# A hybrid decoder trunk on one core: fixed instruction order in the recurrence, later bank copies, branch tiles split in place, ordered loads in the last branch

## The chip, the cores and the metric

The kernel runs on one core of a Trainium2 chip. The time is device microseconds of one execution; the median of three runs of the kernel before is 1837.7 us (1836.87 to 1839.22). A core has five engines that run at the same time: TensorE (PE: matmuls, with PEld for its weight loads), VectorE (DVE), ScalarE (ACT), GpSimd (POOL) and SyncE (SP, which here issues most of the DMA loads). Each engine works through its own instructions in the order in which they were put; waits between engines go by semaphores.

## What is computed

One layer for 1024 tokens of width 1024, in fp32:

```python
h = rms_norm(x)
P = h @ w_in                       # all branches' inputs and the branch gates
y_a = rwkv7(P[...])                # 8 heads x 64, a recurrence over time
y_b = stick_breaking_attention(P[...])   # 8 heads x 64, causal
y_m = cross_attention(P[...], mem)       # 4 heads x 128, 256 memory tokens
merged = sum_b sigmoid(G_b) * (y_b @ w_branch[b])
x = x + merged @ w_out
x = x + conv_ffn(rms_norm(x))      # up, causal convolution of width 3, SwiGLU, down
```

## The kernel before, in words

**Precision.** Each fp32 operand of a large matmul is split into a high half (an fp32r copy, on ACT) and a low half (the rest, on DVE or POOL), and a product is three matmuls: high with high, high with low, low with high (`mm3`). For weights, `load_w` (L75) loads a 128x1024 tile by SP into one of two "wr" buffers, and `split_raw` (L80) makes the halves: ACT copies (L81), POOL subtracts (L82).

**Two streams.** A main stream (preparation of the recurrence, stick-breaking attention, memory attention, the recurrence `stage2`, then `group_norm`) is woven with a filler stream, the "pump": projections, gates, and the products of branches 1 and 2. Both are Python generators. `weave` (L1771) takes one step of the main stream, then so many of the filler (2.08 in `stage2`, 1.0 in `group_norm`). A filler step is one of the eight (or four) depth steps of a product: six matmuls of 512 columns. So the matmuls of both streams alternate in the traced program.

**What sets the order on an engine.** A planner orders each engine's instructions when the kernel is built, by its own estimates of when each is ready and by a priority that follows the trace. `pinned` (L108) puts an edge from an instruction to the one traced just before it on the same engine. An unpinned instruction in between can be moved forward, and then the pinned one behind it is no longer held behind the pinned ones before it. All matmuls go through `pinned`. Of the others, some do (the recurrence's copies and state updates L530, L538, L548, L550, the norm's squares L580), some do not (gate copies L755 and products L756, branch products L1162, weight splits L81 and L82, all loads).

**The recurrence** (`stage2`, L475) has 16 chunks of 64 tokens, each in three main steps: matmuls for A and a DVE copy per head pair (`v1`, L530); matmuls for W and ACT copies (L538); matmuls for Y and the new state, DVE updates of the state (L548), and eight ACT copies into y (L550). Each chunk takes the four PSUM banks of tag "g"; a chunk's first matmuls need the banks that the chunk before it held until its y copies were done. After chunks 3, 7, 11, 13 and 15 `norm_part` (L567) takes means (L573, L574), squares (L580, sixteen or eight) and normalizations (L589) of the finished part between the steps.

**Filler items.** `proj_item` runs eight depth steps into two of the four "mm" banks, and `fin` copies the banks out in the same step as the last six matmuls. For a gate (`gate_item`, L749) `fin` is two ACT copies (L755) and a DVE product (L756) on a tile of tag "w4"; the sigmoid and the store to `gsd` come with a later item (`close_gates`). `branch_item` (L1141) loads a stored gate and, for branch 2, the sum so far (`mrd`), both into "w4" tiles, runs four depth steps, multiplies (L1162), adds, and stores the sum. `load_y` (L1111) loads a branch's four input tiles `yd` into "w4" tiles (L1118), splits them in hooks of a gate item (depth steps 3 to 6: ACT L1129, DVE L1130), the high halves into "inst", the low halves into tiles of tag "A". Tag "w4" has three buffers, "A" four, "at" seven, "qk" eight.

**Attention.** `sb_attn` (scores L848, a scan L854, transposes, copies L866) starts with the first head pair, whose k and q are prepared by `sb_qk`, some of it in hooks of the gate item after q: `k_split(1)` at depth step 1, `q_ss` (norm factors `nf`) at 3, `q_split` at 4 and 6.

**The last branch** (`branch_last`, L1183) has no filler: eight items of 24 matmuls, on the group-normed y. Item d uses half of the branch weights `w_br[0, d // 2]`, its gate (`gsd`, L1197, an "at" tile) and the sum so far (`mrd`, L1198, a "w4" tile), both traced one item ahead. DVE multiplies (L1220), adds (L1225) and makes low halves (L1232) of the merged tiles "mg", ACT the high halves (L1231). Output weights 0 to 3 (`load_wo`) are traced at items 1 to 4, 4 to 7 in `out_proj`. SP's loads are not pinned here, so the planner sets their order.

The up and down projections (`up_phase`, `down_phase`) take the time from about 1200 us on and are not touched.

Of the kernel before, what the change touches and what calls it, by code (L numbers as in the profile page):

```python
# [50 lines left out]
class Trunk:  # L51
    def __init__(self, ctx, tc, I, out):
        self.ctx, self.tc, self.nc, self.I, self.out = ctx, tc, tc.nc, I, out
        self.uid = 0
        self.pin = False

# [18 lines left out]
    def load_w(self, src):  # L75
        raw = self.pool_wt.tile([128, 1024], F32, name=self.nm("wr"), tag="wr", bufs=2)
        self.nc.sync.dma_start(raw, src)
        return raw

    def split_raw(self, raw, hi, lo):  # L80
        self.nc.scalar.activation(hi, raw, AF.Copy)  # L81
        self.nc.gpsimd.tensor_tensor(lo, raw, hi.bitcast(F32), ALU.subtract)  # L82
        return hi, lo

    def split_w(self, src):
# [21 lines left out]

    def pinned(self, ins):  # L108
        if self.pin:
            self.tc.keep_in_program_order(ins)  # L110

    def mmul(self, *a, **k):
# [454 lines left out]
    def norm_part(self, g0, g1):  # L567
        nc = self.nc
        nm, vs = self.small("hn", [128, 16]), self.small("hn", [128, 16])
        nh = 2 * (g1 - g0)  # L570
        ys = [y[:, g0 * 128 : g1 * 128] for y in self.y]
        for p, y in enumerate(ys):
            nc.vector.tensor_reduce(nm[:, p * nh : (p + 1) * nh], y.rearrange("p (g i) -> p g i", i=64), AX.X, ALU.add)  # L573
        nc.vector.tensor_scalar(nm[:, : 4 * nh], nm[:, : 4 * nh], -1.0 / 64, None, ALU.mult)  # L574
        yield
        groups = [(y[:, j * 64 : (j + 1) * 64], p * nh + j) for p, y in enumerate(ys) for j in range(nh)]
        for i in range(0, 4 * nh, 4):
            for y, j in groups[i : i + 4]:
                junk = self.small("jk", [128, 80], bufs=1)[:, :64]
                self.pinned(nc.scalar.activation(junk, y, AF.Square, bias=nm[:, j : j + 1], accum_out=vs[:, j : j + 1]))  # L580
            yield
        rs = self.small("hf", [128, 16], bufs=4)
        self.rsqrt(rs[:, : 4 * nh], vs[:, : 4 * nh], 4 * nh, 1.0 / 64, 64e-5, g0 == 7)
        yield
        for _ in range(0 if g0 == 7 else 3 if nh == 4 else 2):
# [124 lines left out]
    def proj_item(self, src, fin, hook={}):  # L710
        w = self.split_w(src)
        yield
        out = [self.ps("mm"), self.ps("mm")]
        for k in range(8):
            ks = slice(k * 128, (k + 1) * 128)
            self.mm3(out, [a[:, ks] for a in w], self.xin(k), k == 0, k == 7)
            if k == 4:
                self.close_gates()
            if k in hook:
                hook[k]()  # L720
            if k < 7:
                yield
        fin(out)
        yield

# [23 lines left out]
    def gate_item(self, b, d, hook={}, keep=None):  # L749
        nc = self.nc  # L750

        def fin(pp):
            g = self.t4()
            for h in range(2):
                nc.scalar.activation(g[:, h * 512 : (h + 1) * 512], pp[h], AF.Copy)  # L755
            nc.vector.tensor_tensor(g, g, self.rbc, ALU.mult)  # L756
# [12 lines left out]
    def sb_qk(self, p, out):  # L769
# [4 lines left out]
        def k_fin(pp):  # L774
            kr, sq = self.t4(), self.t4()
            for h in range(2):
                nc.scalar.activation(kr[:, h * 512 : (h + 1) * 512], pp[h], AF.Copy)
            nc.scalar.activation(sq, kr, AF.Square)
            st["k"] = sq, kr
# [23 lines left out]
        def q_fin(pp):  # L803
            qr, sq = self.t4(), self.t4()
            for h in range(2):
                nc.scalar.activation(qr[:, h * 512 : (h + 1) * 512], pp[h], AF.Copy)
            nc.scalar.activation(sq, qr, AF.Square)
            st["q"] = sq, qr
# [16 lines left out]
        w = self.I["w_in"]  # L825
        hooks = {1: lambda: k_split(1), 3: q_ss, 4: lambda: q_split(0), 6: lambda: q_split(1)}
        kq = {4: k_bc, 5: lambda: k_split(0)}
# [198 lines left out]
    def mem_q(self, h, out, hook):  # L1026
# [3 lines left out]
        def fin(pp):  # L1030
            sq = self.t4()
            qhi, qlo = self.t4("qk", F32R), self.t4("qk", F32R)
            for i in range(2):
                hs = slice(i * 512, (i + 1) * 512)
                self.pinned(nc.scalar.activation(qhi[:, hs], pp[i], AF.Copy, scale=self.par("memq")))
                self.pinned(nc.scalar.activation(sq[:, hs], pp[i], AF.Square))
                self.pinned(nc.vector.scalar_tensor_tensor(qlo[:, hs], pp[i], self.par("memq"), qhi[:, hs].bitcast(F32), ALU.mult, ALU.subtract))
# [73 lines left out]
    def load_y(self, b, st):  # L1111
# [3 lines left out]

        def load():
            y = self.t4("w4")
            nc.sync.dma_start(y, self.yd[b, len(ys)])  # L1118
            ys.append(y)

        def first():
            for _ in range(3):
                load()

        def split(k):
            if k == 0:
                st["hi"] = self.pool_a.tile([128, 4, 1024], F32R, name=self.nm("yhi"), tag="inst")
            hi, lo, y = st["hi"][:, k], self.t4("A", F32R), ys[k]
            self.pinned(nc.scalar.activation(hi, y, AF.Copy))  # L1129
            self.pinned(nc.vector.tensor_tensor(lo, y, hi.bitcast(F32), ALU.subtract))  # L1130
            out.append((hi, lo))
            if k == 0:
                load()

# [6 lines left out]
    def branch_item(self, b, d, st, first):  # L1141
# [11 lines left out]
        for k in range(4):  # L1153
            self.branch_mm(d, st["w", d // 2], st["y"], pp, k)
            if k == 1:
                self.close_gates()
            if k < 3:
                yield
        g = st.pop(("g", d))
        for h in range(2):  # L1160
            hs = slice(h * 512, (h + 1) * 512)
            nc.vector.tensor_tensor(g[:, hs], pp[h], g[:, hs], ALU.mult)  # L1162
        if not first:
            (nc.vector if d == 7 else nc.gpsimd).tensor_tensor(g, g, o, ALU.add)
        nc.gpsimd.dma_start(self.mrd[d], g)
        yield

# [15 lines left out]
    def branch_last(self):  # L1183
        nc = self.nc
        self.wo = []
        y = self.yhl
        self.pin = True
        mg = lambda name, shape: self.pool_l.tile(shape, F32R, name=name, tag="l4")
# [5 lines left out]
        def load(d):  # L1194
            if d < 8:
                go[d] = self.t4("at"), self.t4()
                nc.sync.dma_start(go[d][0], self.gsd[0, d])  # L1197
                nc.sync.dma_start(go[d][1], self.mrd[d])  # L1198

# [33 lines left out]
        while rest:  # L1233
            rest.pop(0)()
        self.pin = False

    def out_proj(self):
        nc = self.nc
        for k in range(4, 8):
            self.load_wo(k)  # L1240
        wo = self.wo
# [541 lines left out]
    def run(self):  # L1783
# [72 lines left out]
        self.weave(self.group_norm(), pump, 1.0, 0)  # L1856
        drain(pump)
        self.close_gates()
# [79 lines left out]
```

## Time and profile before

| | |
|---|---|
| runs, median of 3 | 1837.7 us (1836.87 to 1839.22) |
| profiled execution, its own time | 1834.23 us |
| its span, first to last instruction | 1832.5 us |
| PE busy | 1783.7 us, 97% |
| DVE, ACT, POOL busy | 1185.4, 881.4, 770.6 us |
| stages (us from the start) | preparation to 320, stick-breaking attention to about 640, memory attention to 762, branch tiles to 828, recurrence to 1012, group norm to 1045, last branch to 1089, output projection to about 1200, up and down after it |

A row of the waits says which engine's instruction (line, tile that it writes) waited for which, then the total in us, how often, and the longest. A row of the timeline says start and length in us, engine, line, operation, output and inputs, shape, count, and in brackets the idle time before it and what ended it. "SPq" and "ACTq" rows are issues of DMAs. A window row has a stretch, its length, and for each engine the busy time and instruction count; then the granted PE clock as a share of full speed, the DMA engines' busy share, and GB/s. Names are those of the program without buffer numbers: "w" is a "w4" tile, "wr", "wh", "wl" a weight's raw tile and halves, "g" and "mm" PSUM banks.

### The profile page before, as it was taken

What the parts mean: (1) busy time and instruction counts of PE and PEld (TensorE: products, weight loads), DVE (VectorE), ACT (ScalarE), POOL (GpSimd) and SP (SyncE); (2) the same over time, 40 slices, a digit from 0 to 9 for tenths busy, and PEclk for the clock granted to TensorE, in tenths of its full rate; (3) what the DMA queues carried; (4) which work ended last, traced back from release to release, by engine and by line L of the source; (5) the groups of instructions that cost most, each with busy time, mean ns of one, the idle gap of its engine ahead of it and who ended that gap; (6) DMA issues with size and microseconds to landing.
All of it is one profiled execution on the core that took longest, in us unless ns stands there. A gap on an engine that the chain in (4) does not pass through costs nothing.

```text
span 1832.5 us, 27438 instructions
## 1 busy us (share of the span) xinstructions
PE 1783.7 (97%) x10468; PEld 1442.8 (79%) x10468; DVE 1185.4 (65%) x1659; ACT 881.4 (48%) x1665; POOL 770.6 (42%) x441
## 2 busy tenths in 40 slices
PE   8999999999999999999899999989999999999999
PEld 6777778778788887787777878868888888878877
DVE  5657664988987514333534792597776777794596
ACT  5443342564666636534456533454444444444333
POOL 2322343232222452122233350476767767635454
PEclk9999999999999999999999999999999999999999
DMA  4155466111112342467665563323332323395475
GB/s 181 58 172 184 161 195 198 50 41 52 56 50 81 111 143 55 167 212 256 229 230 185 194 220 104 127 68 106 113 106 87 119 95 116 115 334 206 138 248 189
DMA packets 120614, 263.39 MB, mean 144 GB/s; under 512 B 28314, under 2 KB 40858, under 8 KB 120355
## 3 DMA queue, kind: packets, MB, share of 16 engines
q1 hardware_dynamic: 82722, 194.76, 32.3%
q10 hardware_dynamic: 33984, 54.27, 8.1%
q0 software_dynamic: 3776, 12.62, 2.2%
q8 instruction: 82, 1.34, 0.3%
q14 instruction: 50, 0.40, 0.1%
HBM read 180.04 MB, written 81.53 MB: 143 GB/s over the span
## 4 chain that ended last, share of the span: by engine, by line
PE 81%; DVE 10%; issue 4%; ACT 2%; POOL 2%; DMA 1%; ACTq 0%; SPq 0%; DVEq 0%; POOLq 0%
PE mm L113 65%; PE g L113 13%; PE g L106 3%; POOL dw L1679 1%; DVE at L854 1%; DVE it L462 1%; DVE qk L379 1%; DVE qk L381 1%; DVE inst L464 1%; DVE BT L1318 1%; DVE mg L1232 0%; DVE qk L817 0%; DMA at<-scr 0%; DVE g L1474 0%; ACT wh L81 0%
## 5 line engine op out<-in xcount | busy, mean ns | idle before, releaser
L82 POOL TENSOR_TENSOR wl<-wr,wh 128x1024 fp32r<-128x1024 f32 x77 | 196.5, 2552 | 475.0 <-ACT wh L81 464.1
L113 PE MATMUL mm<-xhi,wh 128*128 128x512 f32 x784 | 263.3, 416 | 10.1 <-ACT xhi L182 8.1
L113 PE MATMUL mm<-xlo,wh 128*128 128x512 f32 x784 | 244.7, 393 | 0.3 <-DVE xlo L183 0.3
L113 PE MATMUL mm<-xhi,wl 128*128 128x512 f32 x784 | 243.2, 392 | 0.7 <-POOL wl L82 0.7
L113 PEld LDWEIGHTS mm<-xhi,wl 128*128 128x128 f32 x784 | 147.6, 188 | 34.3 <-POOL wl L82 1.6
L113 PEld LDWEIGHTS mm<-xlo,wh 128*128 128x128 f32 x784 | 147.9, 189 | 33.8 <-DVE xlo L183 1.0
L113 PEld LDWEIGHTS mm<-xhi,wh 128*128 128x128 f32 x784 | 137.2, 190 | 40.1 <-issue 9.1
L81 ACT ACTIVATE wh<-wr 128x1024 fp32r<-128x1024 f32 x77 | 81.4, 1057 | 143.6 <-PE mm L113 87.3
L113 PE MATMUL mm<-dw,da 128*128 128x512 f32 x528 | 121.5, 390 | 2.2 <-DVE da L1678 2.0
L113 PEld LDWEIGHTS mm<-dw,da 128*128 128x128 f32 x528 | 98.8, 188 | 24.3 <-DVE da L1678 3.4
L113 PE MATMUL mm<-BT,l 128*128 128x512 f32 x504 | 117.7, 389 | 0.0
L1679 POOL TENSOR_TENSOR dw<-draw,dw 128x512 fp32r<-128x512 f32 x55 | 81.5, 1488 | 83.3 <-ACT dw L1677 83.2
L113 PE MATMUL mm<-BT,wh 128*128 128x512 f32 x352 | 109.2, 390 | 2.8 <-DVE BT L1318 2.8
L854 DVE TENSOR_TENSOR_SCAN at<-at,at 128x128 f32<-128x128 f32 (+3 forms) x64 | 93.3, 1459 | 26.6 <-ACT at L848 26.4
L113 PEld LDWEIGHTS mm<-BT,l 128*128 128x128 f32 x504 | 94.6, 188 | 19.6
L113 PE MATMUL mm<-B,wh 128*128 128x512 f32 x352 | 108.6, 390 | 1.5 <-DVE p L1508 1.5
L1678 DVE TENSOR_TENSOR da<-draw,da 128x512 fp32r<-128x512 f32 x77 | 65.7, 863 | 57.6 <-ACT da L1676 57.1
L113 PE MATMUL g<-dw,da 128*128 128x512 f32 x396 | 90.9, 390 | 2.1 <-POOL dw L1679 1.1
L1409 POOL TENSOR_TENSOR l<-it,l 128x1024 fp32r<-128x1024 f32 x21 | 51.6, 2459 | 95.5 <-ACT l L1408 95.5
L113 PEld LDWEIGHTS g<-dw,da 128*128 128x128 f32 x396 | 74.2, 188 | 18.3 <-ACT dw L1677 1.4
L1676 ACT ACTIVATE da<-draw 128x512 fp32r<-128x512 f32 x77 | 48.3, 629 | 83.6 <-PE mm L113 38.1
L756 DVE TENSOR_TENSOR w<-w,rbc 128x1024 f32<-128x1024 f32 x24 | 49.8, 2074 | 56.8 <-ACT w L755 55.0
(329 smaller groups left out, 3989.9 us busy)
## 6 DMA issues: line engine op xcount, KB each, us to landing
wr<-in_w_in_dram SPq DMA_DIRECT2D x50, 512.0 KB, 3.7
draw<-actd SPq DMA_DIRECT2D x77, 256.0 KB, 4.3
at<-scr SPq DMA_DIRECT2D x28, 512.0 KB, 6.1
draw<-in_w_down_dram SPq DMA_DIRECT2D x55, 256.0 KB, 4.9
rw<-in_w_up_dram SPq DMA_DIRECT2D x22, 512.0 KB, 3.5
actd<-gall ACTq DMA_DIRECT2D x44, 256.0 KB, 3.4
gsd<-w ACTq DMA_DIRECT2D x20, 512.0 KB, 2.8
wr<-in_w_up_dram SPq DMA_DIRECT2D x20, 512.0 KB, 3.7
```

Of the source, the lines that this page charges most:

```text
L81: self.nc.scalar.activation(hi, raw, AF.Copy)
L82: self.nc.gpsimd.tensor_tensor(lo, raw, hi.bitcast(F32), ALU.subtract)
L106: self.pinned(self.nc.tensor.transpose(out, in_, self.ident[:n, :n]))
L113: self.pinned(self.nc.tensor.matmul(*a, **k))
L379: nc.vector.tensor_tensor(bk4[q, :, first ^ h2], self.c8(x[q, hs]), self.c8(Q[q, hs]), ALU.mult)
L381: nc.vector.scalar_tensor_tensor(ra4[:, :, 1, 1:64], self.c8(P[:, hs])[:, :, 0:63], -1.0, self.c8(kk[:, hs])[:, :, 1:64], ALU.mult, ALU.mult)
L756: nc.vector.tensor_tensor(g, g, self.rbc, ALU.mult)
L854: self.pinned(nc.vector.tensor_tensor_scan(sn[:, :W][:, ::-1], sn[:, :W][:, ::-1], self.smask[:, 1024 - W :][:, ::-1], 1.0, ALU.mult, ALU. ...
L1409: keep(eng.tensor_tensor(lo, src, hi.bitcast(F32), ALU.subtract))
L1676: self.pinned(nc.scalar.activation(A[:, 0], a, AF.Copy))
L1678: self.pinned(nc.vector.tensor_tensor(A[:, 1], a, A[:, 0].bitcast(F32), ALU.subtract))
L1679: nc.gpsimd.tensor_tensor(Wt[:, 1], w, Wt[:, 0].bitcast(F32), ALU.subtract)
```

## The change

- `strict`, on in `stage2` and `group_norm`: each pinned instruction is also put behind the last pinned one of its engine. The norm's reductions (L573, L574) and the branch products (L1162) become pinned.
- While `strict` is on, an item's `fin` (bank copies and products) is traced one filler step later, ahead of the next item's first matmuls; the number of filler steps stays.
- `load_y` loads all four tiles at once into "A" tiles and splits in place: the low half overwrites the raw tile. No "w4" tile is used.
- In stick-breaking and memory attention (`guard`), a weight's high half (L81) is put behind the last traced bank copy.
- For the first head pair, `q_ss` moves from depth step 3 to 1 and `k_split(1)` from 1 to 3.
- In `branch_last` all SP loads (branch weights, gates, merged sums, output weights) are pinned in traced order, and output weights 4 to 7 are traced at its end rather than in `out_proj`.

```diff
-        self.pin = False
+        self.pin = self.strict = self.pin_load = False
+        self.last_fixed = {}
+        self.last_fin, self.guard = None, False
...
     def load_w(self, src):
         raw = self.pool_wt.tile([128, 1024], F32, name=self.nm("wr"), tag="wr", bufs=2)
-        self.nc.sync.dma_start(raw, src)
+        self.pinned(self.nc.sync.dma_start(raw, src), self.pin_load)
         return raw
 
     def split_raw(self, raw, hi, lo):
-        self.nc.scalar.activation(hi, raw, AF.Copy)
+        ins = self.nc.scalar.activation(hi, raw, AF.Copy)
+        self.behind(ins, self.last_fin)
         self.nc.gpsimd.tensor_tensor(lo, raw, hi.bitcast(F32), ALU.subtract)
         return hi, lo
+
+    def leave(self, ins):
+        if self.guard:
+            self.last_fin = ins
...
-    def pinned(self, ins):
-        if self.pin:
+    def pinned(self, ins, also=True):
+        if self.pin and also:
             self.tc.keep_in_program_order(ins)
+            if self.strict:
+                self.behind(ins, self.last_fixed.get(ins.ins.engine))
+            self.last_fixed[ins.ins.engine] = ins
+        return ins
+
+    def behind(self, ins, prev):
+        if prev is not None:
+            self.tc.add_manual_dep(
+                ins.ins, prev.ins.name,
+                mybir.DependencyInfo(mybir.DependencyClass.NoSync, mybir.DependencyReason.DATA), reason="fixed order")
...
-            nc.vector.tensor_reduce(nm[:, p * nh : (p + 1) * nh], ...)
-        nc.vector.tensor_scalar(nm[:, : 4 * nh], nm[:, : 4 * nh], -1.0 / 64, None, ALU.mult)
+            self.pinned(nc.vector.tensor_reduce(nm[:, p * nh : (p + 1) * nh], ...))
+        self.pinned(nc.vector.tensor_scalar(nm[:, : 4 * nh], nm[:, : 4 * nh], -1.0 / 64, None, ALU.mult))
...
-            if k < 7:
+            if k < 7 or self.strict:
                 yield
         fin(out)
-        yield
+        if not self.strict:
+            yield
...
-                nc.scalar.activation(g[:, h * 512 : (h + 1) * 512], pp[h], AF.Copy)
+                self.leave(nc.scalar.activation(g[:, h * 512 : (h + 1) * 512], pp[h], AF.Copy))
...
-        hooks = {1: lambda: k_split(1), 3: q_ss, 4: lambda: q_split(0), 6: lambda: q_split(1)}
+        ks, ss = (1, 3) if p else (3, 1)
+        hooks = {ks: lambda: k_split(1), ss: q_ss, 4: lambda: q_split(0), 6: lambda: q_split(1)}
...
-        def load():
-            y = self.t4("w4")
-            nc.sync.dma_start(y, self.yd[b, len(ys)])
-            ys.append(y)
-
         def first():
-            for _ in range(3):
-                load()
+            for k in range(4):
+                ys.append(self.t4("A", F32R))
+                nc.sync.dma_start(ys[k].bitcast(F32), self.yd[b, k])
 
         def split(k):
...
-            hi, lo, y = st["hi"][:, k], self.t4("A", F32R), ys[k]
-            self.pinned(nc.scalar.activation(hi, y, AF.Copy))
-            self.pinned(nc.vector.tensor_tensor(lo, y, hi.bitcast(F32), ALU.subtract))
-            out.append((hi, lo))
-            if k == 0:
-                load()
+            hi, y = st["hi"][:, k], ys[k]
+            self.pinned(nc.scalar.activation(hi, y.bitcast(F32), AF.Copy))
+            self.pinned(nc.vector.tensor_tensor(y, y.bitcast(F32), hi.bitcast(F32), ALU.subtract))
+            out.append((hi, y))
...
             if k == 1:
                 self.close_gates()
-            if k < 3:
-                yield
+            yield
         g = st.pop(("g", d))
...
-            nc.vector.tensor_tensor(g[:, hs], pp[h], g[:, hs], ALU.mult)
+            self.pinned(nc.vector.tensor_tensor(g[:, hs], pp[h], g[:, hs], ALU.mult))
...
-        yield
...
-        self.pin = True
+        self.pin = self.pin_load = True
...
-                nc.sync.dma_start(go[d][0], self.gsd[0, d])
-                nc.sync.dma_start(go[d][1], self.mrd[d])
+                self.pinned(nc.sync.dma_start(go[d][0], self.gsd[0, d]))
+                self.pinned(nc.sync.dma_start(go[d][1], self.mrd[d]))
...
-        self.pin = False
-
-    def out_proj(self):
-        nc = self.nc
         for k in range(4, 8):
             self.load_wo(k)
+        self.pin = self.pin_load = False
+
+    def out_proj(self):
+        nc = self.nc
...
+        self.guard = True
         need("sb0")
         self.weave(self.sb_attn(qk, need), pump, 1.03, 0)
         need("kv")
         self.weave(self.mem_attn(mq, need), pump, 1.6, 0)
         need("mem")
+        self.guard, self.last_fin = False, None
         st2 = self.stage2()
         next(st2)
         need("y1")
+        self.strict = True
         self.weave(st2, pump, 2.08, 0)
         self.weave(self.group_norm(), pump, 1.0, 0)
+        self.strict = False
```

More of the change, by code (lines that the diff above doesn't have):

```diff
@@ L572, in norm_part @@
         for p, y in enumerate(ys):
-            nc.vector.tensor_reduce(nm[:, p * nh : (p + 1) * nh], y.rearrange("p (g i) -> p g i", i=64), AX.X, ALU.add)
-        nc.vector.tensor_scalar(nm[:, : 4 * nh], nm[:, : 4 * nh], -1.0 / 64, None, ALU.mult)
+            self.pinned(nc.vector.tensor_reduce(nm[:, p * nh : (p + 1) * nh], y.rearrange("p (g i) -> p g i", i=64), AX.X, ALU.add))
+        self.pinned(nc.vector.tensor_scalar(nm[:, : 4 * nh], nm[:, : 4 * nh], -1.0 / 64, None, ALU.mult))
         yield
@@ L776, in k_fin @@
             for h in range(2):
-                nc.scalar.activation(kr[:, h * 512 : (h + 1) * 512], pp[h], AF.Copy)
+                self.leave(nc.scalar.activation(kr[:, h * 512 : (h + 1) * 512], pp[h], AF.Copy))
             nc.scalar.activation(sq, kr, AF.Square)
@@ L805, in q_fin @@
             for h in range(2):
-                nc.scalar.activation(qr[:, h * 512 : (h + 1) * 512], pp[h], AF.Copy)
+                self.leave(nc.scalar.activation(qr[:, h * 512 : (h + 1) * 512], pp[h], AF.Copy))
             nc.scalar.activation(sq, qr, AF.Square)
@@ L1035, in fin @@
                 self.pinned(nc.scalar.activation(qhi[:, hs], pp[i], AF.Copy, scale=self.par("memq")))
-                self.pinned(nc.scalar.activation(sq[:, hs], pp[i], AF.Square))
+                self.leave(self.pinned(nc.scalar.activation(sq[:, hs], pp[i], AF.Square)))
                 self.pinned(nc.vector.scalar_tensor_tensor(qlo[:, hs], pp[i], self.par("memq"), qhi[:, hs].bitcast(F32), ALU.mult, ALU.subtract))
@@ L1234, in branch_last @@
             rest.pop(0)()
-        self.pin = False
+        for k in range(4, 8):
+            self.load_wo(k)
+        self.pin = self.pin_load = False
     def out_proj(self):
         nc = self.nc
-        for k in range(4, 8):
-            self.load_wo(k)
         wo = self.wo
```

## The prediction

> **What bounds the kernel.** I read the page first, then who TensorE (PE) waits for, the kernel cut into stages, and the timeline at each stall.
>
> ```profile
> span 1832.5 us, 27438 instructions
> PE 1783.7 (97%) x10468; PEld 1442.8 (79%) x10468; DVE 1185.4 (65%) x1659; ACT 881.4 (48%) x1665; POOL 770.6 (42%) x441
> ```
>
> ```profile
> 828.00:1012.00 184.00, 176.94 (x1855) 138.97 (x1856) 74.56 (x216) 94.87 (x362) 57.65 (x33) 0.98 0.64 221
> 1045.00:1089.00 44.00, 44.00 (x196) 36.44 (x195) 37.65 (x46) 18.51 (x30) 22.36 (x9) 1.00 0.78 285
> ```
>
> The second fence is busy time by stage: the stretch, its length, PE, weight loads, DVE, ACT, POOL, then clock, DMA share, GB/s. PE is the bound and idles 48.8 us in all. The change removes no matmul, so it can only move PE's waits. The recurrence (828 to 1012) idles 7.1 us; the last branch (1045 to 1089) idles nothing, so it can only get worse. PE's waits that the change can reach:
>
> ```profile
> PE g L113 <- DVE ys L530: 3.8, 2, 3.0
> PE g L113 <- ACT qk L550: 3.3, 3, 1.8
> PE g L106 <- DVE at L854: 2.2, 2, 1.5
> PE mm L113 <- DVE at L1220: 1.5, 1, 1.5
> PE mm L113 <- ACT w L755: 0.8, 1, 0.8
> PE mm L113 <- ACT w L806: 0.7, 1, 0.7
> ```
>
> **Fixed order in the recurrence.** The timeline around the first stall (start, length, what):
>
> ```profile
> 869.11 0.22 ACT L550 ACTIVATE qk<-g 64x64 f32<-64x64 f32 x1
> 869.57 1.04 ACT L1129 ACTIVATE yhi<-w 128x1024 fp32r<-128x1024 f32 x1
> 872.36 0.22 ACT L550 ACTIVATE qk<-g 64x64 f32<-64x64 f32 x1
> 871.48 0.33 PE L113 MATMUL g<-ys,at 64*64 64x64 f32 x4 [1.76 <-ACT qk L550]
> 872.63 0.33 PE L113 MATMUL g<-ys,at 64*64 64x64 f32 x4 [0.81 <-ACT qk L550]
> 873.00:876.50 3.50, 3.50 (x23) 2.80 (x18) 1.97 (x6) 0.00 (x0) 2.93 (x1) 0.52 0.58 233
> ```
>
> The eight y copies of a chunk (L550, 0.22 us each) release the four "g" banks. They are pinned only behind whatever was traced just before them, so a branch split (L1129) and the norm's squares stand between them, though eight alone would take 1.9 us. With each pinned instruction also behind the last pinned one of its engine, the copies run together, before the next chunk's first matmul. That takes back 1.76 + 0.81 = 2.57 us. The last row shows 3.5 us at clock 0.52 right behind it: another 3.5 x 0.48 = 1.7. Together 4.3 us.
>
> The Trainium skill ("TensorE: Matmul & The Clock Gate", What's actually happening) says that the clock halves after an idle window of some 3.4 us, and advises no gaps over about 3 us. The row differs: two gaps of 2.57 us in sum sufficed. By the rule as worded, stalls of 3 us and less would cost no clock, and the net below would be two windows of gain less and one of loss less: -4.7 + 3.4 - 1.7 = -3.0. I count by the row.
>
> The second stall:
>
> ```profile
> 883.61 0.32 SPq L1118 DMA_DIRECT2D w<-yd  x1
> 889.33 1.22 DVE L1130 TENSOR_TENSOR A<-w,yhi 128x1024 fp32r<-128x1024 f32 x1 [4.98 <-ACT yhi L1129]
> 890.63 1.08 ACT L755 ACTIVATE w<-mm 128x512 f32<-128x512 f32 x2 [1.34 <-DMA qk<-vd]
> 891.75 1.23 DVE L756 TENSOR_TENSOR w<-w,rbc 128x1024 f32<-128x1024 f32 x1 [1.20 <-ACT w L755]
> 893.17 0.87 PE L113 MATMUL g<-ys,qk 64*64 64x64 f32 x16 [3.00 <-DVE ys L530]
> 866.33 0.73 PE L113 MATMUL mm<-xhi,wh 128*128 128x512 f32 x2
> 893.60:897.00 3.40, 3.40 (x17) 2.70 (x14) 0.00 (x0) 2.21 (x9) 0.00 (x0) 0.50 1.03 395
> ```
>
> The fourth raw tile sits in a "w4" buffer (three exist) until L1130 has read it at 890.55. Only then can the gate's bank copy (L755) start; L756 follows, and the recurrence's copy (L530) is queued behind it on DVE. Raw tiles split in place in "A" leave w4 free, and a gate drained a step later no longer stands ahead of the recurrence: 3.00 + 3.4 x 0.50 = 4.7 us. The new loads wait for "A" buffers that branch 1 releases as its last matmuls run, that is, by 866.33, where the gate's begin. The first split is traced behind the gate's fourth filler step, at least 24 matmuls or 5.4 us later; the load of 883.61 had landed when its 1.04 us split, which ended as L1130 began at 889.33, started: 4.7 us. I count no wait; 0 to +4 is the bound, the upper end being that this wait comes back. Two small stalls of this kind:
>
> ```profile
> 992.87 0.33 PE L113 MATMUL g<-ys,it 64*64 64x64 f32 x4 [0.70 <-ACT qk L550]
> 997.90 0.33 PE L113 MATMUL g<-ys,qk 64*64 64x64 f32 x4 [0.79 <-DVE ys L530]
> ```
>
> Both stand behind work out of turn (a gate's product, sixteen normalizations): 1.5 us. The pinned reductions (L573) and branch products (L1162) add nothing of their own; what queues behind them on DVE is the next v1 copy, covered by the two filler steps (twelve matmuls, 2.7 us) that follow.
>
> **Weight splits behind bank copies** (attention stages).
>
> ```profile
> 387.92 1.06 ACT L81 ACTIVATE wh<-wr 128x1024 fp32r<-128x1024 f32 x1 [0.25 <-issue]
> 389.51 0.50 PE L113 MATMUL mm<-xhi,wh 128*128 128x512 f32 x1 [0.66 <-ACT w L806]
> 411.12 0.50 PE L113 MATMUL mm<-xhi,wh 128*128 128x512 f32 x1 [0.77 <-ACT w L755]
> ```
>
> A split of 1.06 us goes first although the bank copies are what PE needs; swapped, both stalls go: 1.4 us. The split comes about 1.1 us later, and its low half is wanted a whole item later. **Hooks of the first head pair:**
>
> ```profile
> 340.07 1.20 ACT L848 ACTIVATE at<-g,nf 128x128 f32<-128x128 f32 x3 [4.15 <-POOL nf L705]
> 343.44 0.33 PE L106 MATMUL g<-kon,at 128*128 128x128 f32 x1 [1.52 <-DVE at L854]
> ```
>
> The scale nf comes two filler steps (2.7 us) sooner, so the first scan and the transpose behind it do too: 1.5 us.
>
> **Last branch's loads in order.** Now SP must issue, as traced: gate 0, merged 0, branch weights 0, gate and merged 1, gate and merged 2, output weights 0, branch weights 1, and so on. Before:
>
> ```profile
> 1037.00 0.33 SPq L77 DMA_DIRECT2D wr<-in_w_br_dram  x1
> 1039.41 2.79 SPq L1197 DMA_DIRECT2D at<-gsd  x4
> 1057.96 0.81 SPq L1198 DMA_DIRECT2D w<-mrd  x2
> 1047.56 1.04 ACT L81 ACTIVATE wh<-wr 128x1024 fp32r<-128x1024 f32 x1
> 1048.68 2.39 POOL L82 TENSOR_TENSOR wl<-wr,wh 128x1024 fp32r<-128x1024 f32 x1 [2.84 <-ACT wh L81]
> 1056.51 0.62 PE L113 MATMUL mm<-qk,wh 128*128 128x512 f32 x2
> 1053.83 1.97 DVE L1225 TENSOR_TENSOR at<-at,w 128x512 f32<-128x512 f32 x2 [0.48 <-DMA w<-mrd]
> 1086.16 1.29 DVE L1220 TENSOR_TENSOR at<-mm,at 128x512 f32<-128x512 f32 x2 [2.47 <-DMA at<-gsd]
> 1092.20 4.77 PE L113 MATMUL mm<-qk,mg 128*128 128x512 f32 x18 [1.53 <-DVE at L1220]
> wr<-in_w_br_dram SPq DMA_DIRECT2D x12, 512.0 KB, 4.4
> ```
>
> The gain: the gate load that kept L1220 waiting 2.47 us comes in turn, and PE's wait of 1.53 us behind it goes.
>
> The loss: branch weights 1 were issued at 1037.00, some 19 us before PE needs them (1056.51). They now stand behind merged 2, whose w4 buffer is free only when item 0's sum (L1225) has read its own, or the last gate has been stored. L1225 ended at 1055.8, having waited 0.48 for merged 0, which now comes early; so merged 2 goes out at about 1055, the weights 0.8 later (two issues of 0.4). A landing of 4.4 gives 1060.2, the high half at 1061.3 (1.04). POOL has output weights 0 ahead of it: twice 2.4 brings the low half to 1065 or later. PE wants the high half at 1056.5 (1058 with the next term) and the low half four matmuls, 0.9 us, later. That is 4 us for the high half and 3 more for the low: 7, between 3.8 (POOL takes the branch weights first) and 9.8 (the buffer is free only at 1057.96, as the row had it). Like the stall at 893 it should draw a slow window: 1.7 more.
>
> Branch weights 0 stand behind gate 0, which waits for a buffer until about 1038 to 1039.4: plus 0.8, 4.4, 1.0 and 2.4 is 1046.6 to 1048, against the low half's 1046.5. The bounds are 0 and 2.8 (a landing a microsecond or so slower); I take 1.5. For items 4 and 6 the same chain (item d-3's sum, merged d, weights) ends near PE's need, since PE has been delayed itself: 0, at most 4. Output weights 4 to 7 are wanted 13 us into the next stage: nothing, with the same buffers.
>
> **Sum**: gains 4.3 + 4.7 + 1.5 + 1.4 + 1.5 + 1.5 = 14.9; losses 7.0 + 1.7 + 1.5 = 10.2. Net -4.7 on the profiled execution's 1834.23, so 1829.5. That execution lies 3.5 below the median of 1837.7, which gives 1833.0. The likeliest case's own range, from 3.8 + 0 and no slow window up to 9.8 + 1.7 + 2.8: 1826.6 to 1837.1.
>
> **Rivals.**
> 1. *The last branch never catches up* (slower). Every second item waits for its weights: 9.8 + 1.7 at item 2, 2.8 at the start, 4 + 1.7 at item 4, 2 at item 6 make 22.0, net +7.1: 1844.8. It decides once the branch loses over 14.9. For it: w4 has three buffers and DVE is busy 37.65 of 44 us there. Against: a stalled PE lets DVE release buffers early.
> 2. *The order of the loads costs nothing*: the last gate is stored so early that merged 2 goes out by 1048. Then -14.9 + 1.5 = -13.4: 1824.3. Against: in the row above, merged 2 waited to 1057.96.
> 3. *The recurrence trades its waits.* A fixed order has no way around a late load: split 0 waits for its tile, and the copies queued behind it reach PE. Half of 10.5 stays, net about +0.6 to +5: 1838 to 1843. For it: the DMA share is 1.03 in the window at 893.6.
> 4. *The order was fixed already*: only buffers change; net near 0. Against: the interleaved copies at 869.
>
> **Chances.** Forecast 0.46, rival 1 0.18, rival 2 0.15, rival 3 0.18, rival 4 0.03. A measurement of this kernel tells about 0.2% (3.7 us) from no change. Below 1834 lie 0.30 of the forecast's 0.46 and rival 2: faster 0.45. Within: 0.14 of the forecast, 0.08 of rival 3, rival 4: same 0.25. Slower: 0.02, rival 1's 0.18, 0.10 of rival 3: 0.30. The range, 1823 to 1844, takes in rivals 2 and 3 and the near side of rival 1.
>
> **What would show it.** After: no PE wait on L550 or L530 over 1 us in the recurrence and no slow clock there; y copies in one row of eight; L755 not waiting for a buffer; the splits at 388 and 409 behind the copies. In the last branch, SP's branch weights 1 behind three merged loads, and PE idle for 4 us or more at item 2, ended by the weights' halves (L81, L82). The prediction is wrong if the last branch stays at full busy time, or if the recurrence idles as much as before under other names.

## The result: slower by 0.6%, and the profile after

The changed kernel takes 1848.7 us (median, 1846.63 to 1849.77), the kernel before 1838.1 beside it: the ratio is 1.006, 95% interval 1.0048 to 1.0072. That is 10.6 us slower where 4.7 us faster was forecast, and above the top of the range (1844). What follows reads the profiled execution after (1849.77 us, span 1848.0) against the one before (1834.23, span 1832.5). They differ by 15.5 us, more than the medians: the one after is 1.1 above its median, the one before 3.9 below its own.

The page of the changed kernel, its head and the busy times of the engines:

```profile
span 1848.0 us, 27432 instructions
PE 1795.6 (97%) x10468; PEld 1451.0 (79%) x10468; DVE 1174.6 (64%) x1659; ACT 882.0 (48%) x1665; POOL 767.2 (42%) x441
```

PE is "busy" 12 us longer with the same 10468 matmuls. The granted clock accounts for it: PE is busy for 34.4 us at half clock after and for 10.1 before, and half of the difference is 12.2. Where these stretches lie comes below. Since the matmuls run in the same order in both kernels (24 near 325 us, which the hooks move, aside), each can be set beside itself. The start of a matmul after, less its start before, is +3.0 by the end of the preparation (320 us of before), whose code the change leaves alone, and still +2.7 when the recurrence starts (828). It falls to -7.1 by the end of the recurrence (1012), rises to +14.9 by the end of the last branch (1095), and is +15.5 at the end.

The same stages of the changed kernel by busy time (length, PE, weight loads, DVE, ACT, POOL, clock, DMA share, GB/s):

```profile
828.00:1012.00 184.00, 183.27 (x1924) 144.33 (x1923) 75.45 (x225) 101.73 (x380) 60.66 (x35) 1.00 0.67 231
1035.00:1100.00 65.00, 50.49 (x182) 38.86 (x181) 33.23 (x45) 21.14 (x33) 22.19 (x9) 0.84 0.60 219
```

The recurrence, which idled 7.1 us at clock 0.98, idles 0.7 at clock 1.00. The last branch, which idled nothing, idles 14.5, at 0.84 of the clock. PE's waits of both stages after:

```profile
PE mm L130 <- ACT wh L83: 11.4, 3, 4.8
PE mm L130 <- POOL wl L85: 3.2, 3, 2.4
PE g L130 <- DVE ys L547: 0.5, 1, 0.5
```

L83 makes a weight's high half, L85 its low half. The timeline of the last branch after, cut to what made these waits (start, length, then the idle time in brackets):

```profile
1032.16 0.38 SPq L79 DMA_DIRECT2D wr<-in_w_br_dram  x1
1040.92 1.06 ACT L777 ACTIVATE w<-w 128x1024 f32<-128x1024 f32 x1 [1.29 <-DVE w L774]
1042.43 1.06 ACT L83 ACTIVATE wh<-wr 128x1024 fp32r<-128x1024 f32 x1 [0.46 <-ACT w L777]
1043.54 2.08 PE L130 MATMUL mm<-qk,wh 128*128 128x512 f32 x4 [4.81 <-ACT wh L83]
...
1045.02 0.32 SPq L1209 DMA_DIRECT2D w<-mrd  x1
1045.96 0.33 SPq L79 DMA_DIRECT2D wr<-in_w_br_dram  x1
1052.08 1.06 ACT L83 ACTIVATE wh<-wr 128x1024 fp32r<-128x1024 f32 x1 [0.29 <-DMA wr<-in_w_br_dram]
...
1057.65 0.33 SPq L1209 DMA_DIRECT2D w<-mrd  x1
1058.08 0.37 SPq L79 DMA_DIRECT2D wr<-in_w_out_dram  x1
1062.14 0.37 SPq L79 DMA_DIRECT2D wr<-in_w_out_dram  x1
1065.82 0.33 SPq L79 DMA_DIRECT2D wr<-in_w_br_dram  x1
1070.86 0.73 PE L130 MATMUL mm<-qk,wh 128*128 128x512 f32 x2 [1.87 <-ACT wh L83]
1074.47 1.22 PE L130 MATMUL mm<-qk,wl 128*128 128x512 f32 x2 [2.41 <-POOL wl L85]
...
1071.69 0.33 SPq L79 DMA_DIRECT2D wr<-in_w_out_dram  x1
1084.58 0.32 SPq L1208 DMA_DIRECT2D at<-gsd  x1
1085.49 0.36 SPq L79 DMA_DIRECT2D wr<-in_w_br_dram  x1
1092.30 1.22 PE L130 MATMUL mm<-qk,wh 128*128 128x512 f32 x2 [4.67 <-ACT wh L83]
```

Four sets of branch weights, four different stories. *Item 0*: its raw tile left at 1032.16, but the high half runs only at 1042.43, on an ACT with little else to do (1.75 us busy in the 3.4 before, in the cells below): it is queued behind the last gate's sigmoid (L777). *Item 2*, the one forecast to wait longest, does not wait at all: merged 2 takes the buffer of the last gate and goes out at 1045.02, when that gate's store has landed, so the weights leave at 1045.96. *Item 4*: the wait for item 0's sum (L1236), forecast for merged 2, comes one load later, at merged 3 (1057.65). Output weights 1 and 2 and then the branch weights stand behind it in SP's order, and both "wr" buffers are held by the output weights until 1065.8. *Item 6*: SP issues nothing for 12.9 us, from 1071.69 to 1084.58, because a gate load waits for an "at" buffer (until the low halves of item 4, L1243, are made), and the weights stand behind it.

Now the clock. The throttle's record changes only on a grid of 3.413 us. Cells of that grid around the three stalls, same columns as the stages above:

```profile
1039.72:1043.13 3.41, 0.00 (x0) 0.00 (x0) 1.17 (x1) 1.75 (x2) 0.00 (x0) 1.00 0.15 60
1043.13:1046.55 3.42, 2.64 (x5) 1.66 (x6) 0.00 (x0) 0.36 (x1) 2.36 (x1) 0.50 0.97 329
1046.55:1049.96 3.41, 3.41 (x9) 2.65 (x8) 0.15 (x1) 0.00 (x0) 0.00 (x0) 0.50 1.02 406
1070.44:1073.85 3.41, 1.19 (x4) 0.67 (x4) 3.41 (x2) 0.37 (x1) 3.41 (x2) 1.00 0.54 186
1073.85:1077.27 3.42, 2.80 (x7) 2.23 (x8) 2.38 (x4) 1.60 (x4) 0.56 (x1) 0.50 0.21 84
1077.27:1080.68 3.41, 3.41 (x10) 2.65 (x9) 0.00 (x0) 0.67 (x1) 2.37 (x1) 0.50 0.02 5
1090.92:1094.33 3.41, 2.03 (x4) 1.16 (x4) 0.28 (x1) 1.94 (x4) 2.01 (x1) 0.50 0.93 315
1094.33:1097.75 3.42, 3.05 (x8) 2.43 (x8) 0.00 (x0) 1.06 (x1) 0.54 (x2) 0.50 0.82 287
```

Each stall draws two cells at half clock, not one. PE is busy 17.3 us in the six cells and does half as much in them: 8.7 us lost. So the last branch costs 14.5 of waits + 8.7 of clock - 1.5 (the gate load's wait, gone) = 21.7, against 21.9 by the matmuls' starts.

### The profile page after: what moved, and what is told of

It is laid out like the page before. It is cut to its first block, busy times and chain, and to the rows that moved or that the text cites. A ratio compares the mean times of both kernels' runs of the same rounds, so it can differ in the third digit from the quotient of the medians.

```text
span 1848.0 us, 27432 instructions
## 1 busy us (share of the span) xinstructions
PE 1795.6 (97%) x10468; PEld 1451.0 (79%) x10468; DVE 1174.6 (64%) x1659; ACT 882.0 (48%) x1665; POOL 767.2 (42%) x441
## 4 chain that ended last, share of the span: by engine, by line
PE 78%; DVE 11%; issue 4%; ACT 3%; POOL 3%; DMA 2%; ACTq 0%; SPq 0%; DVEq 0%; POOLq 0%
PE mm L130 63%; PE g L130 12%; PE g L113 3%; POOL dw L1690 1%; POOL wl L85 1%; DVE at L873 1%; DVE it L479 1%; DVE qk L396 1%; DVE qk L398 1%; DVE BT L1329 1%; DVE inst L481 0%; ACT wh L83 0%; DVE qk L819 0%; DVE qk L606 0%; DMA actd<-gall 0%
## 5 line engine op out<-in xcount | busy, mean ns | idle before, releaser
L85 POOL TENSOR_TENSOR wl<-wr,wh 128x1024 fp32r<-128x1024 f32 x77 | 195.8, 2544 | 463.9 <-ACT wh L83 460.1
L83 ACT ACTIVATE wh<-wr 128x1024 fp32r<-128x1024 f32 x77 | 81.6, 1059 | 89.6 <-PE mm L130 56.1
L130 PEld LDWEIGHTS mm<-dw,da 128*128 128x128 f32 x528 | 98.9, 188 | 23.2 <-DVE da L1689 2.2
L186 POOL TENSOR_TENSOR hf<-rs,half 128x16 f32<-128x16 f32 (+1 forms) x18 | 48.3, 2682 | 90.6 <-DVE rs L183 85.9
```

What stands on the lines that cost most here:

```text
L83: ins = self.nc.scalar.activation(hi, raw, AF.Copy)
L130: self.pinned(self.nc.tensor.matmul(*a, **k))
L186: nc.gpsimd.tensor_tensor(out, t[:, :n], self.half[:, :n], ALU.pow)
```

## The experiments

Each was timed against the kernel before on the same chip; the ratio is to that. Where nothing else is said, the base is the changed kernel.

### 1. The two halves of the change apart

*e1_loads_free*: the changed kernel, with the last branch's loads as before.

```diff
-        self.pin = self.pin_load = True
+        self.pin = True
...
-                self.pinned(nc.sync.dma_start(go[d][0], self.gsd[0, d]))
+                nc.sync.dma_start(go[d][0], self.gsd[0, d])
```

(likewise the merged load; output weights 4 to 7 back in `out_proj`)

> The changed kernel with the last branch's part undone (loads not pinned, output weights 4 to 7 traced in the output projection again). Theory: the order of the loads alone costs the last branch some 24 us and the other parts take some 10 off, so this runs at 1826 to 1829 us with no PE wait over 1 us in the last branch. Rival (the fixed order and the later bank copies push late work into the last branch, the loads are only where it shows): 1840 us or more, and PE still waits for weight halves there.

*e2_loads_alone*: the kernel before, with only the last branch's loads pinned and output weights 4 to 7 moved.

> The kernel before with the last branch's part alone (its loads pinned, output weights 4 to 7 traced at its end). Theory: 1855 to 1863 us, the same three waits of PE for the branch weights' halves at items 0, 4 and 6, and the recurrence's two stalls as before. Rival: within 4 us of the kernel before.

Measured: e1 1826.9 us, ratio 0.9951 (0.9935 to 0.9968). e2 1857.9 us, ratio 1.0119 (1.0104 to 1.0134). The matmuls' starts of e1 gain 9.7 us in the recurrence and lose 0.1 in the last branch; those of e2 gain nothing in the recurrence and lose 22.7 in the last branch, by the same waits, at the same three items:

```profile
1050.98 2.08 PE L115 MATMUL mm<-qk,wh 128*128 128x512 f32 x4 [4.81 <-ACT wh L83]
1079.58 0.74 PE L115 MATMUL mm<-qk,wh 128*128 128x512 f32 x2 [2.97 <-ACT wh L83]
```

So the whole loss is the loads' order, it does not depend on the faster recurrence ahead of it, and without it the change is worth 8 to 9 us.

### 2. Which load costs it

*e3_weights_free*: gate and merged loads stay pinned, the weights' loads are free (`self.pin_load` stays False).

> The changed kernel with only gate and merged loads pinned in the last branch; branch and output weights may move. Theory (the weights behind loads that wait for buffers are the cost): 1824 to 1830 us. Rival (the pinned gate and merged loads hold SP's queue whatever the weights do): over 1840 us.

*e4_weights_first*: all loads pinned, but each set of branch weights is traced one item sooner, ahead of the gate and merged loads.

```diff
+        ahead = self.split_w(self.I["w_br"][0, 0])
         load(0)
         for d in range(8):
             if d % 2 == 0:
-                w = self.split_w(self.I["w_br"][0, d // 2])
+                w = ahead
+            elif d < 7:
+                ahead = self.split_w(self.I["w_br"][0, d // 2 + 1])
             load(d + 1)
```

> The changed kernel, all loads pinned, but each pair's branch weights are loaded and split one item earlier, ahead of the gate and merged loads that wait for buffers. Theory: the waits at items 0, 4 and 6 go, 1823 to 1830 us. Rival (a fixed order costs whatever it is, since SP stands still at each full buffer): over 1838 us, with waits for output weights or gates instead.

*e5_first_weights_free*: e4, with the load of branch weights 0 alone not pinned.

```diff
-        self.pin = self.pin_load = True
+        self.pin = True
...
         ahead = self.split_w(self.I["w_br"][0, 0])
+        self.pin_load = True
```

> The kernel with weights traced first, but the load of branch weights 0 alone is not held in order. Theory: in the kernel with weights first that load had landed long before (16 us after the stage's start), and the high half ran 25 us later only because an order-held load is planned behind the last gate, so its split was queued behind the last gate's sigmoid. Free, the split runs some 15 us earlier: item 0's waits of 4.81 and 0.45 us go and one slow-clock window of 3.4 to 6.8 us with them: 1834.5 - 5.3 - 1.7 to 3.4 = 1826 to 1828; item 6's wait of 1.9 stays. Rival: the split was late for another reason (ACT full, the buffer of the high half): the wait stays over 3 us and the time 1833 to 1835.

Measured: e3 1834.6 us, ratio 0.9995 (0.9986 to 1.0005). e4 1834.5 us, ratio 0.9996 (0.9986 to 1.0005). e5 1836.4 us, ratio 1.0000 (0.9991 to 1.0010). All three gain the recurrence back and lose it again in the last branch (8.5, 8.7 and 11.4 us there); e3 and e4 stayed above what was expected of them.

e3 shows that it is not the weights' loads alone: with them free, the pinned gate and merged loads still lose 8.5. Gate 0 leaves at 1043.49 (in e1 at 1032.43), and the weights of item 4, free to move, leave at 1056.88 (in e1 at 1047.48). PE waits 1.4 us for a gate's product (L1231), and 4.4 and 1.0 for the halves of item 4's weights:

```profile
1064.83 0.73 PE L130 MATMUL mm<-qk,wh 128*128 128x512 f32 x2 [4.36 <-ACT wh L83]
```

e4 showed what item 0 waits for. Its timeline:

```profile
1008.44 0.33 SPq L79 DMA_DIRECT2D wr<-in_w_br_dram  x1
1039.80 1.06 ACT L777 ACTIVATE w<-w 128x1024 f32<-128x1024 f32 x1 [1.29 <-DVE w L774]
1041.31 1.06 ACT L83 ACTIVATE wh<-wr 128x1024 fp32r<-128x1024 f32 x1 [0.46 <-ACT w L777]
1042.42 1.99 PE L130 MATMUL mm<-qk,wh 128*128 128x512 f32 x4 [4.81 <-ACT wh L83]
```

The load left at 1008.44, 33 us before the split, and PE still waits the same 4.81 us. The transfer was never late; the split has its place in ACT's queue behind the sigmoid. e5 differs from e4 only in that this one load is not pinned. Its timeline:

```profile
1023.70 1.04 ACT L83 ACTIVATE wh<-wr 128x1024 fp32r<-128x1024 f32 x1
1055.36 0.33 SPq L79 DMA_DIRECT2D wr<-in_w_br_dram  x1
1060.06 0.77 PE L130 MATMUL mm<-qk,wh 128*128 128x512 f32 x2 [2.40 <-ACT wh L83]
1077.32 2.79 POOL L85 TENSOR_TENSOR wl<-wr,wh 128x1024 fp32r<-128x1024 f32 x1
1080.16 0.73 PE L130 MATMUL mm<-qk,wl 128*128 128x512 f32 x2 [3.06 <-POOL wl L85]
```

The split moves to 1023.70 and the wait at item 0 is gone, as expected: the pin on a load moves the place that its split gets on another engine. That the planner does this because it reckons a pinned load to start only after what is pinned ahead of it is the likely reason; it was argued, not shown. But the time did not fall, and that expectation failed: PE, no longer held up at item 0, reaches items 4 and 6 sooner and waits there for weights that still stand behind output weights (SP at 1055.36 waits for a "wr" buffer, POOL at 1077.32 comes from an output weight's low half). A wait taken away early in a chain was given back later in it.

*e11_weights_two_ahead*: e5, with every set of branch weights traced one more pair of items sooner, ahead of the output weights that share its two raw buffers. Branch weights 1 are now traced before `pin_load` is set, so weights 0 and 1 are not pinned; all other loads are.

```diff
+        ahead = [ahead, self.split_w(self.I["w_br"][0, 1])]
...
-                w = ahead
-            elif d < 7:
-                ahead = self.split_w(self.I["w_br"][0, d // 2 + 1])
+                w = ahead.pop(0)
+            elif d < 5:
+                ahead.append(self.split_w(self.I["w_br"][0, d // 2 + 2]))
```

> All loads in a fixed order as in the changed kernel, but branch weights 0 and 1 traced ahead of everything (and not held), branch weights 2 and 3 two items earlier than in the changed kernel's trace order plus one, at items 1 and 3, ahead of the output weights that share their two raw buffers. If the cost is in the chosen order (weights behind merged loads and behind output weights), the waits of L83 and L85 all go, with their slow windows, and the gate load's wait too: 1836.4 - 7.5 - 5.1 = 1822 to 1826. If any fixed order of the loads costs (a blocked load holds up those behind it), waits of 2 us or more stay in the last branch: 1829 to 1837.

Measured: 1825.7 us, ratio 0.9938 (0.9921 to 0.9955), as the first theory expected. PE's waits in recurrence and last branch are down to two:

```profile
PE mm L130 <- DVE at L1236: 0.7, 1, 0.7
PE g L130 <- DVE ys L547: 0.4, 1, 0.4
```

The last branch is 0.8 us shorter than before, 22.7 less than after. So a fixed order of gates, merged sums, output weights and branch weights 2 and 3 costs nothing here. What cost was that the order followed the source, where a load is written where its data is used. That weights 0 and 1 are free cannot be the whole of it, since with all weights free e3 lost 8.5; a run with them pinned as well was not made, and e4 speaks against pinning weights 0. The trace has SP issue branch weights 2 and 3 at 1047 and 1056 in e1, at 1041 and 1058 in e11, for items that start at 1059 and 1070; after, at 1065.8 and 1085.5 for items that PE was ready for at 1069.0 and 1087.6.

### 3. The recurrence's three edits, each undone in e1

*e6_no_fixed_order*: pinned instructions are again only behind whatever was traced just before them.

```diff
-            if self.strict:
-                self.behind(ins, self.last_fixed.get(ins.ins.engine))
-            self.last_fixed[ins.ins.engine] = ins
```

> The kernel with the last branch's loads free, less the chain of pinned instructions: branch tiles still split in place, gates still leave a step later. Theory of the prediction: the y copies (L550 of before) are interleaved with splits and squares again; the first stall comes back with 2.6 us of waits and 1.7 of slow clock, the small ones with up to 1.5: 1826.9 + 4.3 to 5.8 = 1831 to 1833; the second stall (893 of before, DVE ys) stays away. Rival: buffers and steps alone took both stalls away: 1826 to 1828.

*e7_tiles_not_in_place*: `load_y` as before, through three "w4" tiles, with separate low halves.

> The kernel with the last branch's loads free, but branch tiles load through three w4 buffers again, with separate low halves; order fixed, gates a step later. Theory of the prediction: the second stall comes back, 3.0 us and 1.7 of slow clock: 1831 to 1832; with the order fixed the fourth split also holds up the copies behind it: up to 1835. Rival: with gates a step later no bank copy waits for a w4 buffer ahead of the recurrence: 1826 to 1828.

*e8_old_step*: gates and branch products leave at their old step (the `yield`s as before).

> The kernel with the last branch's loads free, but gates and branch products at their old step; order fixed, tiles split in place. Theory of the prediction: the buffer was most of the second stall, so it stays away, and the gate's product ahead of the recurrence's copy costs at most the 1.2 us of that product here and there, with no slow window: 1827 to 1829. Rival: in a fixed order the gate's product stands ahead of the recurrence's copy every time, its wait reaches TensorE in several steps and draws slow clock: 1831 to 1837.

Measured: e6 1835.8 us, ratio 0.9992 (0.9983 to 1.0002), above the 1831 to 1833 that was expected. e7 1831.9 us, ratio 0.9972 (0.9962 to 0.9982). e8 1827.2 us, ratio 0.9945 (0.9928 to 0.9962). By the matmuls' starts the recurrence gains 9.7 us in e1, and -0.2, 5.7 and 9.0 in these three. The fixed order is needed for all of the gain: without it the old stall is back, and a worse one further on takes what the buffers saved. The timeline of e6:

```profile
870.68 0.33 PE L127 MATMUL g<-ys,at 64*64 64x64 f32 x4 [1.75 <-ACT qk L564]
991.75 0.33 PE L127 MATMUL g<-ys,it 64*64 64x64 f32 x4 [3.38 <-ACT qk L564]
```

In the changed kernel the same copies run in rows of eight, of which this is the first here:

```profile
870.09 1.87 ACT L567 ACTIVATE qk<-g 64x64 f32<-64x64 f32 x8
```

Splitting in place is worth 4 us on top. In e7 the stall of 3.0 us does not come back whole. Three small waits, 2.1 us in sum, return behind a fourth tile that loads at 882.54 only; most of the rest are gaps of 0.14 us between the small matmuls of the same rows, too short to be listed as waits:

```profile
882.54 0.32 SPq L1137 DMA_DIRECT2D w<-yd  x1
883.24 1.27 PE L130 MATMUL g<-ys,at 64*64 64x64 f32 x12 [0.46 <-ACT qk L567]
889.43 0.72 PE L130 MATMUL g<-ys,qk 64*64 64x64 f32 x16 [1.04 <-DVE ys L547]
893.66 1.27 PE L130 MATMUL g<-ys,at 64*64 64x64 f32 x12 [0.56 <-ACT qk L555]
```

The later step is worth 0.7 us in the trace (one wait on L547 of 1.4 us comes back), less than its time can tell.

### 4. The attention parts, and the best of them

*e9_attention_undone*: e1 without `guard` and with the hooks as before. *e10_hooks_undone*: e1 with the hooks as before.

```diff
-        ks, ss = (1, 3) if p else (3, 1)
+        ks, ss = 1, 3
```

> The kernel with the last branch's loads free, and both attention parts undone (weight splits not held behind bank copies, hooks of the first head pair as before); the recurrence's part alone is left. The prediction's sizes: 1.4 + 1.5 us come back, 1826.9 + 2.9 = 1829.8. Rival: the new wait of 1.0 us at 329 took most of the gain, and which of the 2 us gaps draws a slow window is chance: 1826 to 1828, with waits at 343, 389 and 411 in the trace again and none at 329.

> The kernel with the last branch's loads free, and the hooks of the first head pair as before (the weight splits stay behind the bank copies). If the wait of 1.0 us at 329 comes from the hooks, it goes and the 1.5 at 343 comes back: 1826.9 + 0.5. If it comes from the splits, it stays and the time is 1828.4.

*e12_best*: e11 with the hooks as before.

> The kernel with branch weights two items ahead, with the hooks of the first head pair as before. The two effects lie in different stages and should add: 1825.65 - 0.6 (the wait of 1.0 at 329 less what returns at 343) = 1825.0, within 1.5 by which gaps draw slow windows. Rival: the interplay moves other waits: 1826.5 or more.

Measured: e9 1826.1 us, ratio 0.9940 (0.9925 to 0.9955). e10 1825.5 us, ratio 0.9938 (0.9923 to 0.9953). e12 1825.0 us, ratio 0.9938 (0.9924 to 0.9951). None of them can be told from e1 or e11 by its time, and the prediction's sizes for e9 (1829.8) failed. In the traces the change's hooks make a wait that was not there:

```profile
328.82 1.10 PE L130 MATMUL g<-kon,w 128*64 128x2 f32 x32 [1.01 <-ACT w L825]
```

It is gone in e9, e10 and e12, so it comes from the hooks: the matmuls that sum the factors' squares now come two filler steps sooner, before the squares (L825) are made. The wait of 1.5 us at 343, which the hooks were to remove, does not come back with the old hooks: e2 and e9 have none there, e10 and e12 have 0.45. It belongs to the one execution of the kernel before, which ran at full clock at 310 us; the other four lost 1.7 us to a half-clock cell there and reached the same place later. Like with like, the new hooks are 0.6 to 1.0 us worse: 1.0 at 329 against 0 to 0.45 with that cell, 2.2 (e7) against 1.5 (before) without it. The splits behind bank copies took away the wait of 0.8 us at 411 and 0.24 of the 0.66 at 389, and 0.24 came back at 404 (e10 against e9). Both parts together are no more than one half-clock cell, and such cells come and go in these stages from trace to trace. By the ratios to the kernel before, e12 beats it by 0.6% and the changed kernel by 1.2%.

## Why the prediction was wrong, step by step

- **Fixed order, tiles in place** (forecast 4.3 + 4.7 + 1.5 = 10.5 gained): right in sum, 9.8 by the matmuls' starts. Both large stalls and their half-clock cells are gone, the copies run in rows of eight. The two do not simply add: order without the tiles gains 5.7 (e7; 5.8 was forecast for its two terms), the tiles on top of it 4.0 (of 4.7), but the tiles without the order nothing in sum (e6). The lateness of the new loads, counted as 0 with +4 at most, was 0. Rival 3 is refuted, and by e6 rival 4.
- **Weight splits, hooks** (1.4 + 1.5): of the splits' term about half is in the traces (0.8), of the hooks' term nothing, and neither shows in time. The hooks' 1.5 rested on a wait that one execution had and e2, with the same code there, has not; what is late next (the squares) had not been asked.
- **Gate load in turn** (1.5): right, the wait is gone; but so it is in e12, without the cost.
- **Last branch's loads in order** (10.2 lost): this is the step that failed; 23.2 were lost (14.5 of waits, 8.7 of clock). The kind of wait, the lines (L83, L85) and the engine were as forecast, the place was not. *Item 2* (7.0 + 1.7) cost nothing: merged 2 did not wait for item 0's sum until 1055 but took the last gate's buffer at 1045.02. The forecast wait came at merged 3. *Item 0* (1.5, at most 2.8) cost 5.2 + 3.0: the sum looked at when the tile would land, not at where its split would stand in ACT's queue. *Items 4 and 6* ("0, at most 4") cost 4.3 + 3.1 and 5.0 + 2.5. The sentence that a late PE gives the weights time was the mistake: SP's order ties them to buffers that PE's own progress frees, so a later PE makes later loads. The two raw buffers shared with output weights, and the "at" buffers behind which SP stood for 12.9 us, were not in the sum at all; rows of the queue past item 2 were never written down.
- **Clock** (1.7 for a stall): right for the two stalls of the recurrence; in the last branch each stall drew two cells, 2.5 to 3.1 us.

The gains were 9.8 + 1.5 = 11.3 and not 14.9, so the net is 11.9 lost; the medians say 10.6.

Rival 1, "the last branch never catches up" with 22.0 lost, came nearest in kind, and had been given a chance of 0.18. That its sum is so near is luck: it put 11.5 at item 2, which lost nothing, and 10.5 at items 0, 4 and 6, which lost 23.2. The condition of rival 2 came true (merged 2 out by 1048), but not its outcome, because the wait had only moved to merged 3. The reason held against rival 1 (a stalled PE lets DVE release buffers early) did not decide anything: merged 2 went out early because a gate was stored.

## What to carry to other kernels

Before loads are put in a fixed order, write the whole queue down to its last entry, with the buffer that each load needs and whose progress frees it; a load that stands behind one that waits for the consumer's own progress will be late at every turn. If the order is fixed, trace weights a tile or two ahead, about where the free schedule had them, rather than where the source uses them. Pinning of compute copies that release PSUM banks paid, pinning of loads in the order of the source did not: they are not the same edit. And a wait of a microsecond or two that one profile shows should be looked for in a second one before a gain is counted from it.

## What the runs showed of the hardware that was not expected

The granted clock changes only at multiples of 3.413 us, on a grid that runs through the whole execution (all half-clock cells of one trace lie on it to 0.003 us), and where a stall lies on that grid decides what it costs. A cell of the kernel before and the one that follows it, then the same of e1:

```profile
101.71:105.12 3.41, 1.57 (x11) 1.40 (x12) 3.41 (x5) 0.91 (x2) 0.27 (x1) 1.00 0.19 57
105.12:108.53 3.41, 3.41 (x17) 2.79 (x16) 1.48 (x5) 2.44 (x3) 3.16 (x2) 1.00 1.01 355
```

```profile
100.04:103.45 3.41, 1.15 (x7) 0.67 (x6) 2.20 (x5) 1.15 (x1) 0.00 (x0) 1.00 0.47 169
103.45:106.87 3.42, 3.42 (x13) 3.03 (x13) 1.50 (x3) 1.20 (x2) 1.60 (x1) 0.50 0.50 175
```

A wait of 2.3 us at 101 to 103 us is in both kernels. Before, a cell boundary cuts it and its cell idles 1.84: full clock follows. In e1 it lies in one cell, which idles 2.26: half clock follows. Counted over the traces of all fourteen kernels, of cells at full clock that idled 1.9 us or more, all 32 were followed by half clock, of those between 1.7 and 1.9 13 of 20, of those between 1.2 and 1.7 one of 81: the border is at about half a cell. And a cell that is already slow is followed by another if it idles again: nine such cells idled 0.37 to 2.06 us, and of those that idled less none was (nor was one other of 0.37). That is why each stall of the last branch costs two cells: the end of its waits falls into the cell that their beginning slowed, which idles 0.78, 0.61 and 1.37 us in the three. The Trainium skill ("TensorE: Matmul & The Clock Gate", What's actually happening) gives a free-running window of 3413 ns, which the grid agrees with, and half clock after an idle window; here half an idle window is enough. Its advice against gaps over some 3 us (same page, Why this matters for your kernels) is too lenient here: waits of 2 us cost a cell as well.

One thing stays open. Fourteen more cells idled nothing and were still followed by half clock: one at about 308 us in twelve of the fourteen kernels, one at about 616 in two. Both are stretches of small matmuls (64 of the 71 in the first cell below write four columns or fewer). In the changed kernel:

```profile
309.27:312.68 3.41, 3.41 (x71) 3.09 (x71) 2.16 (x5) 3.38 (x5) 1.35 (x1) 1.00 0.02 5
312.68:316.09 3.41, 3.41 (x10) 2.65 (x9) 1.88 (x1) 0.95 (x1) 3.30 (x2) 0.50 0.46 168
```

The kernel before has 71 matmuls of the same kind there, and full clock after them. Of the profiled execution after, this cell and those at 104 and 620 have no counterpart in the one before. At 1.7 us each they are 5.1, more than the 2.7 by which PE was late at the start of the recurrence. No run was made to find the cause.
